# Hybrid decoder step: short TensorE products of the first stage moved apart in a hand-written order table

## The chip, the cores and the metric

The kernel runs on one core of one Trainium2 chip. The metric is device time in microseconds (us), from the first to the last instruction with what lies around them; lower is better. A core has TensorE (matrix products; PE in the rows, its weight loads PEld), VectorE (DVE), ScalarE (ACT), GpSimd (POOL) and SyncE (SP, which here issues transfers). Each engine carries out its own instructions in their order and waits for other engines at semaphores.

## The reference

One layer of a decoder step for a prompt of 2048 tokens and 8 sample tokens, width 1024, cut to what is computed:

```python
xn = _rmsnorm(x, norm1_g)
z = jnp.einsum('btd,de->bte', xn, w_in)
xr, gr, q, k, v = jnp.split(z, IN_SPLITS, axis=-1)
xc, new_conv = _causal_conv(xr, conv_buf, conv_w, conv_b)
hs, h_last = _rglru(xc, h0, gate_a_w, gate_a_b, gate_x_w, gate_x_b, lru_lambda)
rec = hs * jax.nn.gelu(gr)
att = _prompt_attention(q, k, v, attn_sinks)      # window of 128 tokens, softmax with a sink per head
mix = jnp.concatenate([_rmsnorm(rec, rec_norm_g), _rmsnorm(att, attn_norm_g)], axis=-1)
h = x + jnp.einsum('bte,ed->btd', mix, w_out)
hn = _rmsnorm(h, norm2_g)
ff = jax.nn.silu(hn @ w_gate) * (hn @ w_up)
y = _rmsnorm(h + ff @ w_down, final_norm_g)
```

All in float32; the outputs also hold the last keys and values and the last states.

## The kernel before

**Two stages.** The first stage, roughly the first 660 us, does everything up to `mix` and the output projection; the second does the SwiGLU part. Data lies transposed: 128 features on the partitions, tokens along a row. The tokens come in four blocks s = 0 to 3; block 0 has 520 columns (two products of 260), the others 512. Float32 precision comes from splitting both factors into a high and a low part and from three products for each 128 features:

```python
mm(key, out, wh, xh, start=first, stop=False)
mm(key, out, wh, xl, start=False, stop=False)
mm(key, out, wl, xh, start=False, stop=last)
```

**Large products.** `ip{s}_{u}_{i}` is the input projection of block s, column group u; `op{s}_{m}_{i}` the output projection; `o{block}_{kv}_{i}` the attention output. They read 512 columns (260 for s = 0). `g` are the gate products, `s` the attention scores (256 columns).

**Small products.** For each attention block of 128 tokens and each key/value head, `attn_item` makes four scores tiles, the softmax on VectorE and ScalarE (tile `sc`), and then one or two tiles `pt{block}_{kv}_{kb}`, each of **four** 128x128 transposes (helper `tr`, L401) in the one PSUM buffer of `t_tile`. ScalarE casts such a tile (`pth`, L984), VectorE subtracts (`ptl`, L985), and the products `o` read both. So the next `pt` tile can be written only when `ptl` of the one before is done. The other small products are `st_*` (sums for the norms, `rstd_cols`), `bc_*` (their broadcast back, `row_bcast`), `vt` (transposes of V), `dS` (the sample tokens) and `hb`. They share one more PSUM buffer, `m_tile`. Between `st` and `bc` of a norm, VectorE adds a constant (L453) and GpSimd takes a power (L454): the tiles `rccols`, `atcols`. `mix3_0` is the first normed feature group of block 3, written high part first (ScalarE, L868), low part after (VectorE, L869).

**What sets the order.** TensorE's order in the first stage, and a little beyond it, is a table of names, `PE_ORDER`: an entry `key:n` means the next n products of that key. `order_pe` chains them one behind the other, whatever a product waits for, so a product that waits holds all behind it:

```python
for run in PE_ORDER.split():
    key, _, n = run.partition(":")
    for _ in range(int(n or 1)):
        seq.append(todo[key].pop(0))
for a, b in zip(seq, seq[1:]):
    behind(b, a)
```

Entries that begin with `w_` are filler products (`ones` in the rows). The order of the other engines is chosen when the program is built, by a scheduler that simulates all engines with TensorE's order given; seven pairs in `AFTER` are fixed by hand.

Of the kernel before, what the change touches and what calls it, by code (L numbers as in the profile page):

```python
# [120 lines left out]
ip0_2_1:6 s0_1_0:4 s0_1_1:4 ip0_2_1:2 g0_0_0_260 ip0_2_1:13 pt0_0_1:4 ip0_2_1 s1_0_0:4 ip0_2_1:2 ip0_5_0:3 s1_0_1:4
ip0_5_0 g0_0_1_0 ip0_5_0:9 o0_0_0 ip0_5_0:11 ip0_5_1 s1_1_0:4 ip0_5_1:2 pt0_1_1:4 o0_0_0 ip0_5_1:4 g0_0_1_260
ip0_5_1:12 s1_1_1:2 o0_1_0 s1_1_1:2 ip0_5_1:5 ip0_4_0:6 s2_0_0:4 ip0_4_0:3 o0_1_0 ip0_4_0:11 pt1_0_0:4 ip0_4_0:2
s2_0_1:4 ip0_4_0:2 ip0_4_1:24 ip1_8_0:15 ip0_6_0:2 o1_0_0 ip0_6_0:8 pt1_0_1 o1_0_0 pt1_0_1:3 ip0_6_0 ip1_8_0
g0_3_0_0 ip0_6_0:13 ip0_6_1 ip1_8_0:2 ip0_6_1:15 o1_0_1 g0_3_0_260 s2_1_0:4 ip0_6_1 ip1_8_0 ip0_6_1 pt1_1_0
ip0_6_1:5 o1_0_1 s2_1_1:4 pt1_1_0:3 ip0_6_1 ip1_8_0:5 ip1_9_0 g0_3_1_0 ip1_9_0:19 ip0_7_0:9 ip1_9_0:2 pt1_1_1 o1_1_0
pt1_1_1:3 g0_3_1_260 ip1_9_0:2 ip0_7_0:2 o1_1_0 ip0_7_0:13 w_bc_x1_0 bc_x1_0 s3_0_0:3 s3_0_1:4 ip0_7_1 s3_0_0
ip0_7_1 o1_1_1:2 bc_x1_0 w_pt2_0_0:4 ip0_7_1 bc_x1_0 ip0_7_1 bc_x1_0 ip0_7_1:2 pt2_0_0:4 ip0_7_1:18 ip1_10_0:2
o2_0_0:2 pt2_0_1:3 g0_2_0_0 ip1_10_0:12 pt2_0_1 ip1_10_0:10 ip1_11_0:2 o2_0_1 ip1_11_0 s3_1_0:4 pt2_1_0:4 g0_2_0_260
ip1_11_0 s3_1_1:4 ip1_11_0:2 o2_0_1 ip1_11_0:11 g0_2_1_0 pt2_1_1:3 ip1_11_0:7 ip1_4_0:4 o2_1_0 ip1_4_0 pt2_1_1  # L130
ip1_4_0 o2_1_0 g0_2_1_260 ip1_4_0:18 ip1_0_0:2 o2_1_1 ip1_0_0 vt1_0 ip1_0_0:6 dS:2 o2_1_1 pt3_0_0:4 ip1_0_0:5 dS:6
ip1_0_0:6 o3_0_0 ip1_0_0:4 ip1_12_0:2 dS2:2 ip1_12_0:2 pt3_0_1 o3_0_0 ip1_12_0:2 pt3_0_1:3 ip1_12_0:18 ip1_13_0:6
o3_0_1 ip1_13_0:2 o3_0_1 ip1_13_0:3 pt3_1_0:4 ip1_13_0:9 dS3 ip1_13_0 dS3 ip1_13_0:3 ip1_1_0:8 pt3_1_1:2 o3_1_0
pt3_1_1 ip1_1_0:2 pt3_1_1 o3_1_0 dS4:4 s4_0_0 ip1_1_0:2 o3_1_1 s4_0_1:3 s4_0_0:3 s4_0_1 dS4:4 ip1_1_0 o3_1_1
ip1_1_0:11 ip1_5_0:6 dS5:2 s4_1_0:2 s4_1_1:4 ip1_5_0 vt1_1 ip1_5_0:3 s4_1_0:2 ip1_5_0:8 pt4_0_0:2 ip1_5_0 pt4_0_0:2
ip1_5_0:5 ip1_2_0:2 s5_0_0:4 ip1_2_0 s5_0_1:4 ip1_2_0 vt1_2 ip1_2_0:8 o4_0_0 ip1_2_0:6 pt4_0_1 o4_0_0 pt4_0_1:3
ip1_2_0:3 vt1_3 ip1_2_0:3 o4_0_1 s5_1_0:4 s5_1_1:4 o4_0_1 st_rc0 pt4_1_0:4 st_rc0:4 ip1_6_0:15 pt4_1_1:4 bc_rc0_0:3
s6_0_0:4 bc_rc0_0 s6_0_1 ip1_6_0:4 s6_0_1:3 pt5_0_0 bc_rc0_4 pt5_0_0:3 g1_0_0_0 g1_0_1_0 w_st_at0:13 ip1_6_0
st_at0:5 ip1_6_0:4 ip1_3_0:24 ip1_7_0:3 bc_at0_0:4 ip1_7_0:18 bc_at0_4 ip1_7_0:3 op0_0_0:12 op0_0_260:8 g1_1_0_0
op0_0_260:4 op0_1_0:12 op0_0_0 op0_0_260 op0_1_0 op0_0_260:2 op0_0_0:3 op0_1_0:6 op0_0_0:6 op0_1_0:3 op0_0_260:9  # L140
g1_1_1_0 op0_0_0:2 op0_1_0:2 o4_1_0:2 op0_1_260:4 o4_1_1:2 op0_1_260:20 op0_2_0:11 pt5_0_1:4 o5_0_0:2 op0_2_0:13
op0_2_260:13 s6_1_0:3 s6_1_1:4 s6_1_0 op0_2_260:4 o5_0_1 op0_2_260:7 op0_3_0 w_g1_2_0_0:5 g1_2_0_0 pt5_1_0
op0_3_0:12 o5_0_1 op0_3_0:2 pt5_1_0:3 op0_3_0:9 op0_3_260:17 g1_2_1_0 op0_3_260:7 op0_4_0:24 op0_4_260:6 pt5_1_1:4
op0_4_260:2 o5_1_0:2 op0_4_260:16 op0_5_0 o5_1_1 op0_5_0:11 s7_0_0:4 op0_5_0:3 o5_1_1 op0_5_0:4 s7_0_1:4 pt6_0_0:2
op0_5_0:5 op0_5_260:5 pt6_0_0:2 op0_5_260:12 g1_3_0_0 op0_5_260:7 op0_6_0:10 o6_0_0 op0_6_0:3 pt6_0_1 o6_0_0
pt6_0_1:3 op0_6_0:5 g1_3_1_0 op0_6_0:6 op0_6_260:11 s7_1_0 o6_0_1 pt6_1_0:4 s7_1_1:2 op0_6_260 s7_1_1:2 o6_0_1
op0_6_260:2 s7_1_0:3 op0_6_260:10 op0_7_0:24 op0_7_260:3 o6_1_0 bc_x2_0:3 pt6_1_1 o6_1_0 bc_x2_0 op0_7_260 pt6_1_1:3
op0_7_260:11 o6_1_1 op0_7_260:9 ip2_4_0:24 o6_1_1 ip2_0_0:5 pt7_0_0:4 ip2_0_0:10 st_h0:5 ip2_0_0:2 o7_0_0 ip2_0_0:4
o7_0_0 ip2_0_0:3 ip2_5_0:4 pt7_0_1 st_rc1:2 pt7_0_1:3 st_rc1:2 ip2_5_0:9 pt7_1_0:4 ip2_5_0:2 o7_0_1 ip2_5_0:3 o7_0_1
bc_rc1_0:4 ip2_5_0:3 o7_1_0 ip2_5_0:3 pt7_1_1:3 ip2_1_0:2 pt7_1_1 ip2_1_0:8 g2_0_0_0 ip2_1_0:8 o7_1_0 ip2_1_0:4  # L150
o7_1_1 ip2_1_0:2 o7_1_1 g2_0_1_0 ip2_8_0:24 ip2_12_0:18 g2_1_0_0 ip2_12_0:6 ip2_9_0:23 g2_1_1_0 ip2_9_0 ip2_10_0:24
ip2_11_0:18 vt2_0 ip2_11_0:6 ip2_2_0:7 vt2_1 ip2_2_0:17 ip2_13_0:6 vt2_2 ip2_13_0:18 ip2_7_0:7 vt2_3 ip2_7_0:17
ip2_3_0:5 s8_0_0:4 s8_0_1:4 ip2_3_0:2 w_o8_0 ip2_3_0 st_at1:4 ip2_3_0:16 ip2_6_0 s8_1_0:4 s8_1_1 bc_at1_0:4 s8_1_1
pt8_0_0:2 s8_1_1 pt8_0_0 s8_1_1 pt8_0_0 ip2_6_0:7 s9_0_0:4 ip2_6_0:10 g2_2_0_0 ip2_6_0 o8_0_0 s9_0_1:4 ip2_6_0:5
op1_0_0:5 pt8_0_1 op1_0_0:2 o8_0_0 pt8_0_1:3 op1_0_0:4 g2_2_1_0 op1_0_0:13 op1_1_0:3 o8_0_1 op1_1_0:6 s9_1_0:4
op1_1_0:4 s9_1_1:3 op1_1_0 o8_0_1 op1_1_0:5 pt8_1_0:4 s9_1_1 op1_1_0:5 op1_2_0:24 op1_3_0:6 o8_1_0:2 g2_3_0_0
pt8_1_1:4 op1_3_0:18 op1_4_0 g2_3_1_0 op1_4_0:3 o8_1_1 s10_0_0:4 o8_1_1 s10_0_1 pt9_0_0:2 s10_0_1:3 pt9_0_0:2
op1_4_0:20 op1_5_0:3 pt9_0_1:4 op1_5_0 o9_0_0:2 op1_5_0:16 o9_0_1 op1_5_0:4 op1_6_0:2 bc_x3_0:2 s10_1_0 bc_x3_0:2
s10_1_0:3 op1_6_0:2 o9_0_1 op1_6_0 s10_1_1:4 op1_6_0 pt9_1_0:2 op1_6_0:3 pt9_1_0:2 op1_6_0:5 ip3_8_0 op1_6_0 ip3_8_0
op1_6_0 ip3_8_0 op1_6_0 ip3_8_0 op1_6_0 ip3_8_0 op1_6_0 ip3_8_0 op1_6_0 ip3_8_0 op1_6_0 ip3_8_0 op1_6_0 ip3_8_0  # L160
op1_6_0 o9_1_0 op1_6_0 ip3_8_0 pt9_1_1 o9_1_0 ip3_8_0:5 pt9_1_1:3 ip3_8_0:9 op1_7_0 o9_1_1 s11_0_0:3 pt10_0_0:2
op1_7_0:8 s11_0_0 pt10_0_0:2 o9_1_1 s11_0_1 st_rc2:4 s11_0_1 op1_7_0:2 s11_0_1:2 op1_7_0:7 bc_rc2_0:4 op1_7_0:6
ip3_12_0 o10_0_0 ip3_12_0:3 o10_0_0 pt10_0_1:4 ip3_12_0:12 o10_0_1 ip3_12_0:3 s11_1_0:3 ip3_12_0:5 ip3_10_0:8
s11_1_1:4 pt10_1_0 st_h1:4 pt10_1_0:3 s11_1_0 ip3_10_0:4 o10_0_1 ip3_10_0:3 hb_0_0:4 ip3_10_0:6 o10_1_0 ip3_10_0:3
ip3_9_0 pt10_1_1 o10_1_0 pt10_1_1:3 ip3_9_0:8 hb_0_1:4 ip3_9_0:6 o10_1_1 ip3_9_0:9 ip3_11_0:2 o10_1_1 ip3_11_0
# [1564 lines left out]
```

## Time and profile before

| what | value |
|---|---|
| time, median of 3 runs | 2063.03 us (2059.93 to 2065.46) |
| span of the profiled execution | 2054.6 us |
| median of the runs less that span | 8.4 us |
| TensorE, busy share of the span | 98% |
| TensorE, weight loads | 93% |
| VectorE, ScalarE, GpSimd | 71%, 46%, 44% |
| mean granted clock of TensorE | 0.997 |

The profiled execution has no time of its own beside its span, so the 8.4 us are taken as what lies around the span, with a spread of the runs of about 3 us to either side. A busy TensorE is not TensorE at its peak: the ends of its products are modelled, and the starts of the rows are what a distance is read from.

### The profile page before, as it was taken

To read this page: it belongs to the slowest core of one execution; us is meant where nothing else is said; L and a number is where in the kernel's file an instruction comes from. 1 tells how busy PE (TensorE), PEld (TensorE's weight loads), DVE (VectorE), ACT (ScalarE), POOL (GpSimd) and SP (SyncE) were. 2 spreads that over 40 slices of the span, in tenths; PEclk is the share of its full clock that TensorE was granted. 3 is DMA by queue.
4 is the path that set the end of the run, shared out by engine and by line. 5 is a ranking of instruction groups with operands and counts; after the bars stand their busy time and mean duration, and the time that the engine had idled before them with its cause. 6 is when DMAs were issued, how large, how long until landed. Compare 5 with 4: busy or idle time off the path is not lost.

```text
span 2054.6 us, 34857 instructions
## 1 busy us (share of the span) xinstructions
PE 2015.9 (98%) x12319; PEld 1908.1 (93%) x12319; DVE 1459.9 (71%) x2694; ACT 944.6 (46%) x1960; POOL 906.5 (44%) x799
## 2 busy tenths in 40 slices
...
GB/s 329 293 213 143 188 275 159 175 233 210 208 261 280 314 200 223 205 210 207 207 172 210 229 260 258 227 229 221 222 253 265 211 251 189 183 197 196 197 179 96
DMA packets 208991, 450.98 MB, mean 219 GB/s; under 512 B 25232, under 2 KB 82720, under 8 KB 208800
## 3 DMA queue, kind: packets, MB, share of 16 engines
...
## 4 chain that ended last, share of the span: by engine, by line
PE 77%; DVE 9%; DMA 6%; ACT 3%; issue 2%; POOL 1%; SPq 0%; DVEq 0%; ACTq 0%; POOLq 0%
PE ps_u L396 19%; PE ps_g L396 19%; PE pw L396 11%; PE pd L396 10%; PE ip L396 10%; PE op L396 4%; DMA n<-hs 3%; DMA xs<-in_xT 1%; DMA m<-mixed 1%; PE o L396 1%; PE pt L401 1%; DVE sc L974 1%; DVE sc L963 1%; PE s L396 1%; DMA mixed<-n 1%
## 5 line engine op out<-in xcount | busy, mean ns | idle before, releaser
L396 PE MATMUL ps_g<-hn,w_g 128*128 128x342 f32 (+1 forms) x2772 | 489.4, 320 | 4.6 <-DVE c_u L1410 1.8
L396 PE MATMUL ps_u<-hn,w_u 128*128 128x342 f32 (+1 forms) x2772 | 479.9, 319 | 1.9 <-ACT c_u L1436 1.3
L396 PEld LDWEIGHTS ps_g<-hn,w_g 128*128 128x128 f32 x2772 | 445.1, 188 | 6.0 <-DVE c_u L1410 2.3
L396 PEld LDWEIGHTS ps_u<-hn,w_u 128*128 128x128 f32 x2772 | 444.2, 188 | 2.6 <-ACT c_u L1436 1.6
L396 PE MATMUL ip<-xn,w_in 128*128 128x512 f32 (+1 forms) x1680 | 353.4, 358 | 1.9 <-ACT xn L431 1.8
L396 PEld LDWEIGHTS ip<-xn,w_in 128*128 128x128 f32 x1680 | 270.1, 189 | 46.0 <-issue 3.8
L1500 DVE TENSOR_TENSOR y<-y,pw 128x342 f32<-128x342 f32 x504 | 238.7, 504 | 73.0 <-PE pw L396 72.2
L396 PE MATMUL pd<-fh,w_d 128*128 128x344 f32 (+1 forms) x960 | 239.4, 320 | 0.6 <-DVE y L1469 0.6
L396 PE MATMUL op<-mix,w_out 128*128 128x512 f32 (+1 forms) x960 | 203.4, 357 | 0.5 <-DVE rrec L763 0.3
L396 PEld LDWEIGHTS op<-mix,w_out 128*128 128x128 f32 x960 | 155.4, 188 | 29.3 <-issue 5.0
L1469 DVE TENSOR_TENSOR y<-y,pd 128x344 f32<-128x344 f32 (+1 forms) x240 | 117.9, 507 | 75.3 <-PE pd L396 70.7
L396 PEld LDWEIGHTS pd<-fh,w_d 128*128 128x128 f32 x960 | 168.3, 188 | 1.4 <-DVE y L1469 1.1
L396 PE MATMUL pw<-fh,wd 128*128 128x342 f32 x576 | 165.6, 319 | 1.2 <-DVE y L1500 1.2
L396 PE MATMUL pd<-fl,w_d 128*128 128x344 f32 (+1 forms) x480 | 153.4, 320 | 0.0
L1381 DVE TENSOR_TENSOR fl<-c_u,fh 128x342 fp32r<-128x342 f32 (+1 forms) x132 | 107.1, 815 | 48.3 <-ACT fh L1380 47.9
L1225 POOL TENSOR_TENSOR w_u<-ru,w_u 128x512 fp32r<-128x512 f32 x44 | 58.9, 1338 | 181.6 <-ACT w_u L1224 155.0
L1392 POOL TENSOR_TENSOR c_u<-c_u,c_g 128x342 f32<-128x342 f32 (+1 forms) x60 | 60.5, 1008 | 170.7 <-DVE c_u L1410 132.1
L1380 ACT CAST fh<-c_u 128x342 fp32r<-128x342 f32 (+1 forms) x132 | 63.0, 480 | 157.8 <-POOL c_u L1392 61.9
L396 PE MATMUL pw<-t,wd 128*128 128x342 f32 x648 | 126.7, 320 | 2.6 <-DVE t L1381 1.7
L1410 DVE TENSOR_TENSOR c_u<-c_u,ps_u 128x342 f32<-128x342 f32 (+1 forms) x99 | 50.2, 507 | 100.3 <-PE ps_u L396 100.1
L396 PEld LDWEIGHTS pw<-t,wd 128*128 128x128 f32 x648 | 106.0, 188 | 4.4 <-DVE t L1381 2.5
L396 PEld LDWEIGHTS pw<-fh,wd 128*128 128x128 f32 x576 | 105.3, 189 | 1.7 <-DVE y L1500 1.5
...
## 6 DMA issues: line engine op xcount, KB each, us to landing
...
```

Source lines behind the costliest of these rows:

```text
L396: r = nc.tensor.matmul(*args, **kw)
L401: r = nc.tensor.transpose(*args)
L963: seen[f"sm{gb}_{kv}_{g}"] = nc.vector.tensor_tensor_reduce(sc[:, g, :kn], ps[:, gi * 256:gi * 256 + kn], mask[:, k0:k0 + kn], -SCALE, ns[ ...
L974: nc.vector.tensor_scalar(sc[:, g, :kn], sc[:, g, :kn], mx[:, 1, g:g + 1], None, ALU.mult)
L1225: lo_eng.tensor_tensor(w[:, 1, :], src, w[:, 0, :].bitcast(F32), op=ALU.subtract)
L1380: nc.scalar.copy(hi, v)
L1381: nc.vector.tensor_tensor(lo, v, hi.bitcast(F32), ALU.subtract)
L1392: (nc.vector if p == NPAIR - 1 or src is not v else eng(E_MUL[2 * h + n])).tensor_tensor(v, src, g, op=ALU.mult)
L1410: nc.vector.tensor_tensor(o, a, b, op)
L1469: r = nc.vector.tensor_tensor(ys[gi, n, m], ys[gi, n, m], ps, ALU.add)
L1500: nc.vector.tensor_tensor(v, v, ps, ALU.add)
```

## The change

Only the string `PE_ORDER` differs; it grows by 24 lines, so that every later line number is 24 higher in the changed kernel (L396 becomes L420, L401 becomes L425). No instruction is added or removed, and the order of the 3072 large products among themselves stays. Where several small products stood behind one another, the first stays where it is and each of the others goes behind one of the following large (or score or gate) products. Two lines of the table, before and after:

```diff
...
-pt11_0_0:4 ip3_11_0:16 vt3_0 ip3_11_0:5 ip3_13_0:3 pt11_0_1 o11_0_0:2 ip3_13_0 pt11_0_1:3 ip3_13_0:4 vt3_1
...
+ip3_9_0 hb_0_1 ip3_9_0 hb_0_1 ip3_9_0 hb_0_1 ip3_9_0:3 o10_1_1 ip3_9_0:9 ip3_11_0:2 o10_1_1 ip3_11_0 pt11_0_0 ip3_11_0
+pt11_0_0 ip3_11_0 pt11_0_0 ip3_11_0 pt11_0_0 ip3_11_0:13 vt3_0 ip3_11_0:5 ip3_13_0:3 pt11_0_1 o11_0_0:2 ip3_13_0
...
```

Counted from the two tables: 213 small products move later, behind 1 to 8 further large ones (132 transposes of `pt`, 13 `s`, 36 `st`, 15 `bc`, 11 `dS` and 6 `hb`). The places where a small product follows a small one fall from 631 to 454, so 177 are pulled apart. Of the 62 `pt` tiles, 51 have their last transpose later: by one large product in 10, two in 23, three in 11, four in 5, five in 2.

First place, TensorE in block 3 (a name's last number is a buffer number; `ip_11_0` is `ip3_11_0`, `pt_0_0` is `pt11_0_0`), before:

```order
L396 MATMUL o_1_5216<-ptl_1_1_5213,vt_2_4067 128x512
L396 MATMUL ip_11_0_5227<-xn_0_4656,w_in_11_0_5143 128x512
L401 MATMUL pt_0_0_5312<-cs,sc_0_5286 128x128 x4
L396 MATMUL ip_11_0_5227<-xn_1_4661,w_in_11_0_5143 128x512 x3
L396 MATMUL ip_11_0_5227<-xn_2_4666,w_in_11_0_5143 128x512 x3
```

and in the changed kernel:

```order
L420 MATMUL ip_11_0_5227<-xn_0_4656,w_in_11_0_5143 128x512
L425 MATMUL pt_0_0_5312<-cs,sc_0_5286 128x128
L420 MATMUL ip_11_0_5227<-xn_1_4661,w_in_11_0_5143 128x512
L425 MATMUL pt_0_0_5312<-cs,sc_0_5286 128x128
L420 MATMUL ip_11_0_5227<-xn_1_4661,w_in_11_0_5143 128x512
L425 MATMUL pt_0_0_5312<-cs,sc_0_5286 128x128
L420 MATMUL ip_11_0_5227<-xn_1_4661,w_in_11_0_5143 128x512
L425 MATMUL pt_0_0_5312<-cs,sc_0_5286 128x128
L420 MATMUL ip_11_0_5227<-xn_2_4666,w_in_11_0_5143 128x512 x3
```

The run of four transposes has become four single ones; the last of them stands behind three more products of `ip`. This is the commonest form of the change.

Second place, TensorE at the start of the last output projection (full names; `op3_0_0` is the projection of block 3, `st_h2` a norm's sums, `pt15_1_0` a transposed tile of the last attention block), before:

```order
L396 MATMUL op3_2_0_6840<-mix3_0_6289,w_out3_2_0_0_6458 128x512
L396 MATMUL st_h2_6516<-avg_104,hacc2_6025 128x1
L401 MATMUL pt15_1_0_6937<-cs_101,sc15_1_6817 128x128 x4
L396 MATMUL op3_0_0_6468<-mix3_0_6289,w_out3_0_0_0_6406 128x512 x2
L396 MATMUL op3_0_0_6468<-mix3_1_6293,w_out3_0_0_0_6406 128x512 x2
L396 MATMUL st_h2_6516<-avg_104,hacc2_6025 128x1 x3
```

and in the changed kernel:

```order
L420 MATMUL op3_2_0_6840<-mix3_0_6289,w_out3_2_0_0_6458 128x512
L420 MATMUL st_h2_6516<-avg_104,hacc2_6025 128x1
L420 MATMUL op3_0_0_6468<-mix3_0_6289,w_out3_0_0_0_6406 128x512
L425 MATMUL pt15_1_0_6937<-cs_101,sc15_1_6817 128x128
L420 MATMUL op3_0_0_6468<-mix3_0_6289,w_out3_0_0_0_6406 128x512
L425 MATMUL pt15_1_0_6937<-cs_101,sc15_1_6817 128x128
L420 MATMUL op3_0_0_6468<-mix3_1_6293,w_out3_0_0_0_6406 128x512
L425 MATMUL pt15_1_0_6937<-cs_101,sc15_1_6817 128x128
```

The second product of `op3_0_0`, which reads the low part of `mix3_0`, now stands ahead of all four transposes of `pt15_1_0`; before, it stood behind them.

Third place, VectorE near 215 us (`atcols` is the step between the sums and the broadcast of block 0's attention norm, `xc` the convolution, `gt` and `rrec` the gate branch), before:

```order
L842 SCALAR_TENSOR_TENSOR gt_0_2607<-gt_0_2607,rrec 128x512
L453 TENSOR_SCALAR atcols_2792<-st_at_2793 104x5
L786 SCALAR_TENSOR_TENSOR xc_1_2742<-xr_1_2226,vec,xc_1_2742 128x512
L763 TENSOR_TENSOR rrec<-ip_6_0_2859,rb_x_1489 128x512
L786 SCALAR_TENSOR_TENSOR xc_1_2742<-xr_1_2226,vec,xc_1_2742 128x512
L844 SCALAR_TENSOR_TENSOR rrec<-gt_0_2607,rrec 128x512
```

and in the changed kernel:

```order
L866 SCALAR_TENSOR_TENSOR gt_0_2607<-gt_0_2607,rrec 128x512
L810 SCALAR_TENSOR_TENSOR xc_1_2742<-xr_1_2226,vec,xc_1_2742 128x512 x2
L868 SCALAR_TENSOR_TENSOR rrec<-gt_0_2607,rrec 128x512
L787 TENSOR_TENSOR rrec<-ip_6_0_2859,rb_x_1489 128x512
L477 TENSOR_SCALAR atcols_2792<-st_at_2793 104x5
L810 SCALAR_TENSOR_TENSOR xc_1_2742<-xr_1_2226,vec,xc_1_2742 128x512
```

The short step of `atcols` went behind four long ones. Such shifts of single instructions stand all through the first stage on VectorE, ScalarE and GpSimd; the instructions are the same.

## Rows read from the trace of the kernel before

**Rows 1.** The page: the span, and TensorE's busy time.

```profile
span 2054.6 us, 34857 instructions
PE 2015.9 (98%) x12319; PEld 1908.1 (93%) x12319; DVE 1459.9 (71%) x2694; ACT 944.6 (46%) x1960; POOL 906.5 (44%) x799
```

**Rows 2.** Busy time by stretch: each engine's sum over nine stretches, 0 to 700 us.

```profile
sum 700.00, PE 677.70 PEld 575.34 DVE 536.97 ACT 410.68 POOL 198.16; mean PE 75.30 PEld 63.93 DVE 59.66 ACT 45.63 POOL 22.02
```

**Rows 3.** The chain that ended last, from 347 us: start, length, what.

```profile
347.74 10.00 PE ip L396 x43
```

**Rows 4.** Timeline of TensorE, 485 to 492 us: start, length, instruction, count.

```profile
485.45 0.60 PE L401 MATMUL pt<-cs,sc 128*128 128x128 f32 x4
485.81 3.97 PE L396 MATMUL ip<-xn,w_in 128*128 128x512 f32 x16
489.62 0.27 PE L401 MATMUL vt<-cs,vraw 128*128 128x128 f32 x1
489.64 2.11 PE L396 MATMUL ip<-xn,w_in 128*128 128x512 f32 x8
491.59 0.27 PE L401 MATMUL pt<-cs,sc 128*128 128x128 f32 x1
```

**Rows 5.** Timeline of TensorE, 514 to 516 us: single transposes between large products.

```profile
514.63 0.27 PE L401 MATMUL pt<-cs,sc 128*128 128x128 f32 x1
514.66 0.48 PE L396 MATMUL o<-ptl,vt 128*128 128x512 f32 x1
514.98 0.27 PE L401 MATMUL pt<-cs,sc 128*128 128x128 f32 x1
515.32 0.38 PE L401 MATMUL pt<-cs,sc 128*128 128x128 f32 x2
```

**Rows 6.** TensorE's waits to 660 us: for what, us in total, times, longest.

```profile
PE pt L401 <- DVE ptl L985: 3.1, 6, 1.1
PE o L396 <- ACT pth L984: 2.9, 2, 2.1
...
PE o L396 <- DVE ratt L997: 1.2, 2, 0.7
...
PE bc_rc L396 <- POOL rccols L454: 0.7, 1, 0.7
...
PE o L396 <- DVE ptl L985: 0.4, 1, 0.4
```

**Rows 7.** Tile `pth`: what ScalarE idled for ahead of its 62 casts.

```profile
  PE pt L401: 28.8, 21
```

**Rows 8.** Timeline, 425 to 432 us: one `pt` tile and what follows from it.

```profile
425.48 0.38 PE L401 MATMUL pt<-cs,sc 128*128 128x128 f32 x2
...
429.69 0.57 ACT L984 CAST pth<-pt 128x512 fp32r<-128x512 f32 x1
```

**Rows 9.** Timeline, 199 to 202 us: from the sums to the broadcast `bc_rc`.

```profile
199.02 0.15 DVE L453 TENSOR_SCALAR rccols<-st_rc 104x5 f32<-104x5 f32 x1
...
199.25 1.18 POOL L454 TENSOR_TENSOR rccols<-rccols,nhalf 104x5 f32<-104x5 f32 x1 [1.89 <-DVE rccols L453]
...
201.99 0.81 PE L396 MATMUL bc_rc<-cs,rccols 104*128 104x104 f32 x6
```

**Rows 10.** Timeline, 628 to 630 us: transposes of `pt15_1_0`; brackets: idle before, and releaser.

```profile
628.51 0.65 PE L401 MATMUL pt<-cs,sc 128*128 128x128 f32 x4 [0.56 <-DVE ptl L985]
629.10 0.79 PEld L396 LDWEIGHTS op<-mix,w_out 128*128 128x128 f32 x4 [0.18 <-DVE mix L869]
```

**Rows 11.** Timelines, 215 to 224 us: block 0's `atcols` and its broadcast.

```profile
215.77 1.60 POOL L454 TENSOR_TENSOR atcols<-atcols,nhalf 104x5 f32<-104x5 f32 x1 [13.30 <-DVE atcols L453]
...
222.62 1.04 PE L396 MATMUL bc_at<-cs,atcols 104*128 104x104 f32 x8
```

**Rows 12.** By stretch: length, busy us (instructions) of each engine, granted clock, transfers.

```profile
210.00:211.50 1.50, 0.17 (x1) 0.17 (x2) 1.50 (x3) 1.50 (x4) 0.00 (x0) 0.78 0.00 0
211.50:213.00 1.50, 1.50 (x8) 1.50 (x9) 1.50 (x4) 1.50 (x4) 0.00 (x0) 0.50 0.00 0
```

More of the change, by code (lines that the diff above doesn't have):

```diff
@@ L121 @@
[L121 to L165, printed above, removed]
@@ L181 @@
-w_op3_0_0:13 op3_0_0 op3_1_0 o15_0_1 op3_2_0 st_h2 pt15_1_0:4 op3_0_0:4 st_h2:3 op3_0_0 o15_0_1 op3_1_0:3 op3_2_0:3
-op3_0_0:3 op3_1_0:3 op3_2_0:3 op3_0_0:3 pt15_1_1 op3_1_0:3 op3_2_0:3 op3_1_0:2 op3_2_0:2 o15_1_0:2 op3_3_0:3
-pt15_1_1:3 op3_3_0:9 op3_4_0:11 o15_1_1:2 op3_4_0 op3_5_0:12 op3_6_0:12 op3_7_0:12 op3_0_1 op3_1_1 op3_0_1:6
-w_op3_3_1:2 op3_1_1 st_at3 op3_1_1 op3_0_1:3 op3_1_1:3 st_at3:3 op3_0_1:2 op3_1_1:6 op3_3_1:10 bc_at3_0:4 op3_3_1:2
-op3_2_1:12 op3_4_1:12 op3_6_1:12 op3_7_1:12 op3_5_1:12 g0_0_1:12 g0_0_2:12 g0_0_5:12 g0_0_6:12 u0_0_1:12 g0_0_7:12
@@ L186 @@
[L186 to L190 removed]
+ip0_1_0:2 ip0_1_1:2 ip0_12_0:2 ip0_12_1:5 ip0_9_0:5 st_x0 ip0_9_0 st_x0 ip0_9_0 st_x0 ip0_9_0 st_x0 ip0_9_0 st_x0
@@ new lines @@
+ip1_2_0 s5_0_1:4 ip1_2_0 vt1_2 ip1_2_0:8 o4_0_0 ip1_2_0:6 pt4_0_1 o4_0_0 pt4_0_1 ip1_2_0 pt4_0_1 ip1_2_0 pt4_0_1
+ip1_2_0 vt1_3 ip1_2_0:3 o4_0_1 s5_1_0:4 s5_1_1:4 o4_0_1 st_rc0 ip1_6_0 pt4_1_0 ip1_6_0 pt4_1_0 ip1_6_0 pt4_1_0 ip1_6_0
+pt4_1_0 ip1_6_0 st_rc0 ip1_6_0 st_rc0 ip1_6_0 st_rc0 ip1_6_0 st_rc0 ip1_6_0:7 pt4_1_1:4 bc_rc0_0:3 s6_0_0:4 bc_rc0_0
+s6_0_1 ip1_6_0:4 s6_0_1:3 pt5_0_0 bc_rc0_4 pt5_0_0:3 g1_0_0_0 g1_0_1_0 w_st_at0:13 ip1_6_0 st_at0 ip1_6_0 st_at0
+ip1_6_0 st_at0 ip1_6_0 st_at0 ip1_6_0 st_at0 ip1_3_0:24 ip1_7_0:3 bc_at0_0 ip1_7_0 bc_at0_0 ip1_7_0 bc_at0_0 ip1_7_0
```

113 lines of the change are left out of this document (90 added, 23 removed).

## The prediction

> **What bounds the kernel now.** I read the page first, then the busy time by stretch, the chain of waits, the timeline of TensorE in several places, TensorE's list of waits, and last the tiles that the moved products feed. The page puts TensorE at 2015.9 of 2054.6 us busy [rows 1], so the kernel ends when TensorE has worked through its table, and a change counts only by what it does to the distance between the starts of TensorE's products. In the stretch that the table covers, TensorE is marked busy for 677.70 of 700 us [rows 2]: 22.3 us at most are open gaps, and part of those lie at the start and behind the first stage. The chain shows the pace: 43 large products in 10.00 us, 0.2326 us each [rows 3].
>
> **What a small product costs, in a run and alone.** This decides whether pulling them apart pays, and the trace before holds both forms. A run: from the first of four transposes at 485.45 to a single `vt` transpose at 489.62 are 4.17 us, in which 4 small and 16 large products start [rows 4]. The 16 large ones take 16 x 0.2326 = 3.72, which leaves 0.45 for four, 0.112 us each. Alone: from that `vt` at 489.62 to the next transpose at 491.59 are 1.97 us with one small and 8 large products [rows 4]; less 1.86 that leaves 0.11. Alone and in the new pattern, one small behind each large: transposes start at 514.63, 514.98 and 515.32 with one 512-column product between each [rows 5]; two pairs in 0.69 us, less 0.465, leave 0.112 us each. So it is 0.11 us every way.
>
> The rows tempt to another reading. Behind the single transpose at 514.63 the large product is marked as starting only 0.03 us later [rows 5], as if the small one had almost vanished. But the next start is 0.32 us behind that, not 0.23: the large product gives back what the small one seemed to save.
>
> The Trainium skill ("TensorE: Matmul & The Clock Gate", Part 2, step 1, on LDWEIGHTS) says that the next product's weights load while the present one streams. By that rule alone a small product behind a large one would cost only its own columns; with the page's spacing of 56 ns for an isolated 128-column product the 177 places would give 177 x (0.112 - 0.056) = 9.9 us, an estimate from that page. The trace agrees that the small one's own load is hidden, and differs on the sum: its pairs keep 0.112.
>
> **The change part by part.**
>
> *Spacing.* 177 places are pulled apart at a difference of 0.112 - 0.112 = 0. The starts are rounded to 0.01 us, so one pair may be off by 0.005, and the bounds are 177 x 0.005 = 0.9 us to either side. I take 0.
>
> *Results that come later.* 51 of the 62 `pt` tiles have their last transpose later, by 10 x 1 + 23 x 2 + 11 x 3 + 5 x 4 + 2 x 5 = 119 large products, 2.33 on the mean or 0.54 us. What reads the tile starts later by that, if its engine was waiting for it. ScalarE idled until a transpose came ahead of 21 of its 62 casts [rows 7]; ahead of the other 41 it was busy, as at 425 us, where the last transposes start at 425.48 and the cast runs at 429.69 [rows 8]. So about a third of the delays are passed on. They reach TensorE only where it already waits for such a result, or nearly. Five kinds of wait hang on the moved products (`pt` on `ptl`, `o` on `pth`, on `ratt` and on `ptl`, `bc_rc` on `rccols`): 6 + 2 + 2 + 1 + 1 = 12 waits, 8.3 us in all [rows 6]. All twelve lengthened by 0.54, a third of the time: 12 x 21/62 x 0.54 = 2.2 us. The other bound is 0, since products that follow a `pt` run in the table may have moved with it, and TensorE then waits less because it has had the same work to do ahead. I take the middle, **+1.1**.
>
> *The place at 628 us.* TensorE waits 0.56 us for `ptl`, does four transposes, then waits 0.18 for the low part of `mix3_0`, and goes on with `op` from 629.10 [rows 10]. In the changed table the second product of `op3_0_0`, which needs that low part, stands ahead of the transposes. They then begin at about 629.1, not 628.51: four small products that lay in the wait now come behind it, 4 x 0.112 = **+0.5** (bounds 0, if VectorE writes the low part earlier in its new order, and 0.6, the whole of 628.51 to 629.10).
>
> *The sums and broadcasts.* At 199 us the ten sums of `st_rc0` move behind up to eight of the 15 `ip` products that follow them, so that 7 large products and 4 transposes are left ahead of the broadcast `bc_rc`: 7 x 0.2326 + 4 x 0.112 = 2.08 us. VectorE's step starts 0.23 ahead of GpSimd's and that one takes 1.18 [rows 9], 1.41 together; with the start of VectorE some tenths behind the last sum it is 1.6 to 1.8 and fits by about 0.3. I cost it at 0; what hides it is those 2.08 us, and a VectorE that is busy for 0.3 us longer would uncover it, 1 for 1.
>
> *The other engines' order.* Their instructions are the same and only stand elsewhere. The largest shift I found near a norm is the VectorE step of `atcols` behind four instructions. Before, GpSimd's power ends at 215.77 + 1.60 = 217.37 and the broadcast starts at 222.62 [rows 11]: 5.25 us of room, so the four would have to take 1.3 us each to make it late. I cost such shifts at 0 and bound them by the waits that they could remove or double, 8.3 us either way [rows 6].
>
> *The clock.* TensorE fell to the half clock once inside the stage, at 211.5 to 213 us, behind a stretch with 0.17 of 1.5 us of work [rows 12]. Another such gap would cost at most some 1.5 us; I see no place where the change opens one, and take 0.
>
> The sum is 0 + 1.1 + 0.5 = +1.6 us on a span of 2054.6; with the 8.4 us between that span and the median of the runs the time is **2064.6 us**, no change that can be told (0.3%, 6.2 us, is about what a measurement of this kernel can tell from none).
>
> **The rivals.**
>
> *The small products do vanish behind the large ones* (faster). For it: the start of the large product 0.03 us behind the transpose [rows 5]. If each separated product cost that and no more, 177 x (0.112 - 0.03) = 14.5 us would go: 2050.1. Against it: the pairs of the same rows. Chance 0.07.
>
> *The new order of VectorE and ScalarE takes the waits away* (faster). All 8.3 us of those twelve waits gone, with the 0.5 of 628 us: 2054.6 + 0.5 - 8.3 + 8.4 = 2055.2. For it: the scheduler places the instructions anew around transposes that come one at a time. Against it: the same instructions on engines that were late for two thirds of the tiles. It must remove 6.7 us of the 8.3 to count as faster. Chance 0.05.
>
> *The later transposes hold the one `pt` buffer* (slower). Each tile's chain is transposes, cast, subtraction, next tile's transposes, all through one buffer, and `o` behind it. If half of the 51 later tiles pass their 0.54 us on to TensorE, that is 26 x 0.54 = 14.0 us: 2054.6 + 14.0 + 0.5 + 8.4 = 2077.5. For it: TensorE already waits for `ptl` in six places [rows 6], and products that wait hold everything behind them in the table. Against it: the 41 tiles for which ScalarE was busy anyway. It decides from (6.2 - 0.5) / 0.54, so 11 tiles on. Chance 0.27.
>
> **How the numbers follow.** My forecast has 0.61, and the rivals 0.07, 0.05 and 0.27. The range goes from the second rival's 2055 to the third's 2077; it leaves out the first rival and the upper part of the third, together about 0.2, and takes in the bounds of the shifts. The forecast by itself would lie in 2059 to 2069. Faster by over 0.3% are the first two and a little of the forecast, 0.13; slower are the third and a little of the forecast, 0.30; within 0.3% is the rest, 0.57.
>
> **What would show it.** Spacing: in the changed trace, single transposes between large products 0.34 to 0.35 us apart, start to start; 0.26 would mean the first rival. Later results: the five kinds of wait at 8 to 11 us in all; over 14, or ScalarE idling for transposes ahead of far more than 21 casts, means the third; under 2 the second. The place at 628: transposes of `pt15_1_0` first behind a wait for `mix`. The sums: no wait of `bc_rc` much over 0.7. The prediction is wrong if the scheduler's new order makes a long wait where there was none, for a norm's columns or a gate, which no row of before can show.

## The result: slower by 0.38%

| | median | runs | ratio to before, 95% interval |
|---|---|---|---|
| before | 2060.89 us | 6 | |
| changed | 2069.11 us | 6 | 1.0038 [1.0026, 1.005] |

The changed kernel is about 7.8 us slower (0.0038 x 2061). That lies inside the range of 2055 to 2077, but it is not the "no change" that I held likeliest: it is just past the 0.3%, on the slow side, with an interval that begins at 0.26%. The profiled execution of the changed kernel (page: span):

```profile
span 2064.9 us, 34858 instructions
```

The span is 10.3 us longer than in [rows 1]. These spans must be read with care. The runs of the changed kernel have both numbers, and the time is 1.8 us above the span in each (2066.69 for this 2064.9). So the 8.4 us that I put around the span of before were wrong: 2054.6 + 1.8 is 2056.4, a quick execution of a kernel whose runs, in this section and the next, went from 2053 to 2066 us (one more, of 2444.94 us, was in the slow state and is left out). The profiled execution of the changed kernel is the quickest of its six.

**Spacing, as forecast.** TensorE's timeline of the changed kernel, where transposes stand one behind each large product:

```profile
518.13 0.27 PE L425 MATMUL pt<-cs,sc 128*128 128x128 f32 x1
518.16 0.48 PE L420 MATMUL ip<-xn,w_in 128*128 128x512 f32 x1
518.48 0.27 PE L425 MATMUL pt<-cs,sc 128*128 128x128 f32 x1
...
518.82 0.27 PE L425 MATMUL pt<-cs,sc 128*128 128x128 f32 x1
```

The transposes start 0.35 and 0.34 us apart, as in [rows 5]: 0.23 for the large product and 0.11 for the small one.

**The place at 628 us, as forecast.** All engines, changed kernel (what answers to [rows 10]):

```profile
636.52 0.28 PE L420 MATMUL st_h<-avg,hacc 128*128 128x1 f32 x2
638.02 0.50 PE L420 MATMUL op<-mix,w_out 128*128 128x512 f32 x1 [1.22 <-DVE mix L893]
638.36 0.27 PE L425 MATMUL pt<-cs,sc 128*128 128x128 f32 x1
639.74 0.28 PE L420 MATMUL st_h<-avg,hacc 128*128 128x1 f32 x2
```

The transposes now come behind one whole wait of 1.22 us for the low part of `mix3_0`. From one row of `st_h` to the next, 636.52 to 639.74, are 3.22 us with five large products and four transposes between. Before, the rows that answer to them were

```profile
627.68 0.28 PE L396 MATMUL st_h<-avg,hacc 128*128 128x1 f32 x2
...
630.14 0.72 PE L396 MATMUL st_h<-avg,hacc 128*128 128x1 f32 x6
```

630.14 - 627.68 = 2.46 us apart, with four large products and four transposes between. Less 0.23 for the fifth, the place costs 0.53 us, forecast 0.5.

**The sums and the broadcast near 200 us, as forecast** (answers to [rows 9]):

```profile
202.77 1.18 POOL L478 TENSOR_TENSOR rccols<-rccols,nhalf 104x5 f32<-104x5 f32 x1 [3.37 <-DVE rccols L477]
204.48 0.81 PE L420 MATMUL bc_rc<-cs,rccols 104*128 104x104 f32 x6
```

GpSimd's power ends at 203.95 and the broadcast starts at 204.48 without a wait.

**The waits.** TensorE's waits of the changed kernel to 680 us, the largest and those that had been watched (columns as in [rows 6]):

```profile
PE s L420 <- DVE mx L987: 4.1, 5, 3.0
PE o L420 <- ACT pth L1008: 2.8, 3, 1.6
PE o L420 <- DVE ptl L1009: 2.3, 2, 1.5
...
PE pt L425 <- DVE ptl L1009: 1.5, 3, 1.1
```

The five kinds of wait that I had watched did not grow: 2.8 + 2.3 + 1.5 and 1.2 of `bc_rc`, together 7.8 against 8.3 in [rows 6] (`o` on `ratt` is no longer among them). What is new is `s` on `mx`: score products that wait for VectorE's score minima, 4.1 us, of which 2.95 at one place (609.66 us), and a new wait of 1.5 for `ptl` at 542.51.

**The two places.** The chain of waits of the changed kernel from 530 us (start, length, what), its longest pieces:

```profile
529.05 4.13 DMA mixed<-n
533.20 4.37 DMA n<-hs
...
537.67 0.58 DVE n L545
538.24 0.61 DVE gt L866
538.88 0.64 ACT gt L867
...
540.15 0.48 DVE sc L987
...
541.85 0.61 DVE ptl L1009
542.51 0.67 PE o L420
```

and from 590 us:

```profile
596.37 4.95 DMA mixed<-n
601.33 3.22 DMA n<-hs
604.65 0.59 DVE n L545
...
605.78 0.61 DVE q L839
606.41 1.06 ACT q L843
607.50 1.29 DVE ix L846 x2
...
609.66 0.51 PE s L420 x2
```

Both begin at the same pair of transfers: the norm ahead of the second stage stores a tile `mixed`, and only then loads the next tile `n` from `hs`. VectorE, in its order, stands at `n` until the load lands (537.67 and 604.65), and the gate step, the minima and `ptl` stand behind it, with ScalarE's cast behind the gate step. SyncE's own timeline shows what changed in the transfers, at both places alike. Before, both stores of a pair stand ahead of a weight load:

```profile
524.68 1.34 SPq L525 DMA_DIRECT2D mixed<-n  x2
526.12 0.38 SPq L380 DMA_DIRECT2D w_in<-split_w  x1
...
589.59 0.87 SPq L525 DMA_DIRECT2D mixed<-n  x2
590.56 0.40 SPq L380 DMA_DIRECT2D w_out<-split_w  x1
```

and in the changed kernel the second store stands behind it:

```profile
528.16 0.32 SPq L549 DMA_DIRECT2D mixed<-n  x1
528.57 0.38 SPq L404 DMA_DIRECT2D w_in<-split_w  x1
529.05 0.41 SPq L549 DMA_DIRECT2D mixed<-n  x1
...
595.48 0.32 SPq L549 DMA_DIRECT2D mixed<-n  x1
595.85 0.42 SPq L404 DMA_DIRECT2D w_out<-split_w  x1
596.37 0.41 SPq L549 DMA_DIRECT2D mixed<-n  x1
```

The weight loads have 512 KB, the store 172. At the first place the second load of `n` is issued 4.15 us behind the second store (529.05 to 533.20); before it was 1.87 (525.71 to 527.58). The profiles of all kernels here, those of the next section too, agree: 1.9 us in each of the seven with both stores ahead of the weight load, 3.8 to 4.2 in each of the seven with the load between them. At the second place the same stretch is 1.9 to 3.5 us with both stores ahead and 4.0 to 5.0 with the load between (e4, with yet another order there, is left out). SyncE's order never changed alone, so this is seen in the traces and not tested by itself.

At the second place the longer store is only a part of it. In the kernel before, the chain and VectorE's timeline have

```profile
590.14 2.73 DMA mixed<-n
...
592.88 4.74 DMA n<-hs
...
597.71 0.58 DVE n L521
...
599.95 0.47 DVE L963 CUSTOM_DVE_ANT_0 sc<-s,cs,nsk 128x256 f32<-128x256 f32 x1
```

and VectorE's timeline of the changed kernel

```profile
608.71 0.48 DVE L987 CUSTOM_DVE_ANT_0 sc<-s,cs,nsk 128x256 f32<-128x256 f32 x1
```

The store took 4.95 us instead of 2.73, but the load behind it 3.22 instead of 4.74. Taken against the 5.9 us by which this execution is behind at 590 us, `n` is worked on about 1.0 us later than before and the first minimum (608.71) 2.9 later. The other 1.8 us are VectorE's own order: the two `ix`, which wait for ScalarE's `q`, now stand ahead of the four minima, so that these begin 4.06 us behind `n` and not 2.24. At the first place, reckoned in the same way, `n` is worked on 1.6 us later than before and the minima begin 2.5 later; the rest is `rrec`, which waits for ScalarE's gate step and now stands ahead of them.

Behind each wait TensorE's granted clock fell to the half level (by stretch, changed kernel):

```profile
543.00:544.50 1.50, 1.50 (x9) 1.50 (x8) 1.26 (x3) 0.22 (x1) 0.00 (x0) 0.50 0.98 343
544.50:546.00 1.50, 1.50 (x8) 1.32 (x8) 1.36 (x5) 0.99 (x2) 0.00 (x0) 0.50 0.50 202
...
611.00:612.50 1.50, 1.50 (x6) 1.30 (x6) 1.50 (x3) 1.49 (x2) 0.19 (x1) 0.50 0.93 359
612.50:614.00 1.50, 1.50 (x5) 1.11 (x5) 1.50 (x3) 1.50 (x6) 0.19 (x1) 0.50 0.76 295
```

Two stretches of 3 us at half clock. An estimate of what each cost is 1.5 us at most, half of its 3 us, since TensorE is busy all through them; the stretch at 211.5 us of [rows 12] is gone.

**Where the time went.** The start of each product in the table, less its start in the profile of before, shows where an execution falls behind. Medians over the large products within 2 us, in us; the last line is the difference of the spans. The other columns are kernels of the next section.

```
time in   changed  table new,  table old,  before  new order  table new but
before             others old  others new  again   mended     for 4 places
                   (e5)        (e6)        (e9)    (e10)      (e11)
   70       0.0      -0.1        -0.2       -0.1     -0.1       -0.4
  216       1.3       2.3         1.4       -0.8      1.2       -0.9
  300       1.5       2.5         0.8       -1.2      0.6       -1.0
  340       2.1       4.9         1.4       -1.2      1.5       -0.8
  500       1.7       5.6         0.1       -1.4      1.1       -0.8
  530       3.1       5.5         0.7       -1.4      1.1       -0.8
  550       7.5       5.6         4.8       -1.6      1.0       -0.8
  590       5.9       5.4         3.2       -1.6      0.1       -0.4
  612      10.3       5.9         8.5       -2.1      0.5       -0.4
  640       9.4       7.8         6.8       -2.7      3.5       -0.1
  696      10.1       8.6         6.7       -2.7      3.5        0.6
  end      10.3      11.6         7.9        0.8      9.5        3.7
```

The column of the kernel before, profiled again, wanders by up to 2.7 us, so a difference of 1 or 2 us between columns shows little. Up to 500 us the changed kernel is 1.7 us behind, which is within that. It loses 4.4 from 530 to 550 and 4.4 from 590 to 612, the two places; e6 loses 4.1 and 5.3 there.

### The profile page after: what moved, and what is told of

Read it like the earlier page. It is cut to its first block, busy times and chain, and to the rows that moved or that the text cites. A ratio compares the mean times of both kernels' runs of the same rounds, so it can differ in the third digit from the quotient of the medians.

```text
span 2064.9 us, 34858 instructions
## 1 busy us (share of the span) xinstructions
PE 2020.3 (98%) x12319; PEld 1908.2 (92%) x12319; DVE 1455.8 (71%) x2694; ACT 946.2 (46%) x1960; POOL 904.7 (44%) x799
## 4 chain that ended last, share of the span: by engine, by line
PE 79%; DVE 9%; DMA 5%; issue 2%; ACT 2%; POOL 2%; SPq 0%; DVEq 0%; ACTq 0%; POOLq 0%
PE ps_u L420 19%; PE ps_g L420 18%; PE pw L420 10%; PE ip L420 10%; PE pd L420 10%; PE op L420 6%; DMA n<-hs 2%; PE s L420 1%; PE g L420 1%; PE o L420 1%; PE pt L425 1%; DMA mixed<-n 1%; DVE sc L987 1%; DVE hn L602 1%; DMA rd<-in_wdown 1%
## 5 line engine op out<-in xcount | busy, mean ns | idle before, releaser
L420 PE MATMUL ps_g<-hn,w_g 128*128 128x342 f32 (+1 forms) x2772 | 489.5, 320 | 5.0 <-DVE xres L1159 2.1
L420 PE MATMUL ps_u<-hn,w_u 128*128 128x342 f32 (+1 forms) x2772 | 479.8, 319 | 1.2 <-DVE c_g L1434 0.7
L420 PEld LDWEIGHTS ps_g<-hn,w_g 128*128 128x128 f32 x2772 | 445.1, 188 | 6.8 <-DVE c_u L1434 2.4
L420 PEld LDWEIGHTS ps_u<-hn,w_u 128*128 128x128 f32 x2772 | 444.0, 188 | 1.9 <-DVE c_g L1434 1.0
L420 PE MATMUL ip<-xn,w_in 128*128 128x512 f32 (+1 forms) x1680 | 371.1, 364 | 1.9 <-ACT xn L455 1.6
L420 PEld LDWEIGHTS ip<-xn,w_in 128*128 128x128 f32 x1680 | 272.7, 190 | 47.5 <-issue 3.9
L420 PE MATMUL pd<-fh,w_d 128*128 128x344 f32 (+1 forms) x960 | 239.5, 320 | 0.3 <-DVE y L1493 0.2
L420 PE MATMUL op<-mix,w_out 128*128 128x512 f32 (+1 forms) x960 | 210.2, 363 | 1.9 <-DVE mix L893 1.2
L420 PEld LDWEIGHTS op<-mix,w_out 128*128 128x128 f32 x960 | 157.0, 189 | 32.7 <-issue 5.3
L420 PEld LDWEIGHTS pd<-fh,w_d 128*128 128x128 f32 x960 | 168.3, 188 | 1.2 <-DVE y L1493 0.9
L420 PE MATMUL pw<-fh,wd 128*128 128x342 f32 x576 | 165.7, 320 | 1.5 <-DVE y L1524 1.5
L420 PE MATMUL pd<-fl,w_d 128*128 128x344 f32 (+1 forms) x480 | 153.4, 320 | 0.0
L420 PE MATMUL pw<-t,wd 128*128 128x342 f32 x648 | 126.5, 320 | 2.9 <-DVE t L1405 2.3
L420 PEld LDWEIGHTS pw<-t,wd 128*128 128x128 f32 x648 | 106.1, 188 | 4.3 <-DVE t L1405 3.4
L420 PEld LDWEIGHTS pw<-fh,wd 128*128 128x128 f32 x576 | 105.3, 189 | 2.2 <-DVE y L1524 2.1
```

Source lines behind the costliest of these rows:

```text
L420: r = nc.tensor.matmul(*args, **kw)
```

## The experiments

Two theories stood against each other. **Theory O**: the loss comes from the order that the scheduler chose anew for the other engines. **Theory T**: it comes from the table itself, from small products that are separated and later. To part them, an engine's instructions can be chained in any order that was read from a built program:

```diff
+PINNED = {
+    "DVE": """
...
+""",
...
+        def pin_all():
+            by = {i.name: i for i in nc.cur_bb.bb.instructions}
+            for run in PINNED.values():
+                seq = [by[f"I-{n}"] for n in run.split() if f"I-{n}" in by]
+                for a, b in zip(seq, seq[1:]):
+                    tc.add_manual_dep(b, a.name, no_sync, reason="issue order")
...
             order_pe()
-            order_engines()
+            pin_all()
```

The changed kernel's order of VectorE, ScalarE, GpSimd and SyncE differs from that of before in 180 short pieces, in which 2 to 11 instructions are permuted. All ratios below are to the kernel before on the same chip. They are estimated from all runs of both, and are not exactly the quotients of the medians. The median of the kernel before was 2060.41 us beside e1 to e4, 2060.12 beside e5 to e8 and 2058.48 beside e9 to e12; so times of different groups are compared by their ratios.

| kernel | median, us | ratio, 95% interval |
|---|---|---|
| e1 table new, others old, minima free | 2068.48 | 1.0042 [1.0027, 1.0057] |
| e2 table old, others new, minima free | 2066.32 | 1.0029 [1.0018, 1.0039] |
| e3 only `pt` pulled apart | 2067.00 | 1.0036 [1.0023, 1.0049] |
| e4 only the rest pulled apart | 2070.26 | 1.0052 [1.0035, 1.0069] |
| e5 table new, all others old | 2067.22 | 1.0029 [1.0017, 1.004] |
| e6 table old, all others new | 2067.24 | 1.0029 [1.0018, 1.0039] |
| e7 changed, four minima first | 2066.86 | 1.0029 [1.0019, 1.0038] |
| e8 changed, minima and cast first | 2066.70 | 1.0030 [1.0019, 1.0041] |
| e9 before again | 2059.63 | 1.0000 [0.9988, 1.0012] |
| e10 changed, two stretches in old order | 2062.28 | 1.0012 [1.0001, 1.0022] |
| e11 others old, table new but for four places | 2061.61 | 1.0015 [1.0004, 1.0026] |
| e12 table old, two stretches in new order | 2061.74 | 1.0011 [1.0001, 1.0021] |

**e1 and e2: the table and the order apart.** Edit: `pin_all` in the changed kernel with the order of before (e1), and in the kernel before with the order of the changed one (e2).

> TensorE has the changed table; the other four engines are held to the order that they had in the kernel before. Theory O (the loss comes from the order that the scheduler chose anew for VectorE, ScalarE and SyncE): within 0.1% of the kernel before, 2060 to 2064 us. Theory T (the separated and later small products cost it themselves): like the changed kernel, 2068 to 2071 us.

> The reverse: TensorE has the table of before, the other four engines are held to the order that they have in the changed kernel. Theory O: like the changed kernel, 2067 to 2071 us, with TensorE waiting over 3 us for VectorE's score minima near 602 us. Theory T: like the kernel before, 2060 to 2063 us.

Both were slower, by 0.42% and 0.29%. Neither theory alone allows that. In e2 TensorE's wait for the minima was 1.79 us, not over 3. The lists of both lacked the 128 score minima on VectorE, whose place the scheduler still chose; in e1 four of them had come behind the two `ix` near 600 us, as in the changed kernel. So the pair was made again, complete, as e5 and e6.

**e3 and e4: half of the table each.** Edit: in the table of before only `pt` is moved as in the change (e3, 132 products), or only `st`, `bc`, `dS` and `hb` (e4, 68 products); the scheduler is free. The 13 score products that the change moves stay as before in both, though the expectation of e4 names them.

```diff
...
-pt11_0_0:4 ip3_11_0:16 vt3_0 ip3_11_0:5 ip3_13_0:3 pt11_0_1 o11_0_0:2 ip3_13_0 pt11_0_1:3 ip3_13_0:4 vt3_1
+o10_1_1 ip3_9_0:9 ip3_11_0:2 o10_1_1 ip3_11_0 pt11_0_0 ip3_11_0 pt11_0_0 ip3_11_0 pt11_0_0 ip3_11_0 pt11_0_0 ip3_11_0:13
...
```

> Only the pt transposes are pulled apart, the rest of the table is that of before; the other engines' order is chosen anew. Theory T: 132 of 213 moved products, so about 5 of the 8 us, 2066 us. Theory O: nothing proportional; what decides is the order that comes out, anywhere from 2058 to 2070 us.

> The other part alone: st, bc, dS, hb and s products pulled apart, the pt transposes in runs as before. Theory T: about 3 of the 8 us, 2064 us, and with the transposes-only kernel it adds up to the 8 us. Theory O: anywhere from 2058 to 2070 us, and the two need not add up.

Each half costs about as much as the whole, 0.36% and 0.52%, and they do not add up to 0.38%. That speaks against a cost for each moved product, and fits theory O or an order that reacts to any change. The profile of e4, taken of the slowest of its six runs, has a wait that no other profile here has: 5.8 us of `o` for `pth`.

**e5 and e6: the pair, complete.**

> As the first of these kernels, but with all of VectorE held to its order of before; there the 128 score minima (L963 of before) had been left to the scheduler, and near 600 us four of them had come behind the two ix products, as in the changed kernel. Theory O (the other engines' order): 2060 to 2064 us. Theory T (the table itself): 2068 to 2071 us. Theory M (table and order of before fit each other, and either one changed alone breaks the fit): 2066 to 2070 us, without the 3 us wait near 605 us.

> The reverse with all of VectorE held to its order in the changed kernel. Theory O: 2067 to 2071 us. Theory T: 2060 to 2063 us. Theory M: 2066 to 2070 us, with waits of TensorE near 540 and 602 us.

Both are 0.29% slower, and the changed kernel, which has both changes, 0.38% [0.26, 0.50]: less than the 0.58% of the two added up. Of the three theories only M gave these numbers, but what it says of a fit is a reading of them; the two columns above show where each kernel loses. e5 loses 0.1 us from 530 to 550 us and 0.5 from 590 to 612: with the old order the two places are gone. It loses instead in steps of about 1 to 2 us where a moved result is late, above all at 80 to 100, 200, 309 to 323 and 612 to 640 us. TensorE's timeline of e5 at two of them:

```profile
85.48 0.47 PE L749 MATMUL o<-pth,vt 128*128 128x512 f32 x1 [0.97 <-DVE ratt L1357]
...
313.46 0.48 PE L749 MATMUL o<-pth,vt 128*128 128x512 f32 x1 [1.27 <-DVE ratt L1357]
```

The first of these waits stood in the kernel before too (0.74 us, at 84.58) and has grown; at the second TensorE had not waited. What ScalarE idled for ahead of its 62 `pth` casts (columns as in [rows 7]) says the same. In the changed kernel:

```profile
  PE pt L425: 34.9, 24
```

and in e5:

```profile
  PE pt L754: 42.5, 28
```

Before it was 28.8 us at 21 tiles. e6 has the old table and still both places, with waits of 1.31 us for `ptl` and 3.96 for `mx`:

```profile
540.06 0.56 PE L725 MATMUL o<-ptl,vt 128*128 128x512 f32 x1 [1.31 <-DVE ptl L1321]
...
607.88 0.39 PE L725 MATMUL s<-KK,qst 128*128 128x256 f32 x1 [3.96 <-DVE mx L1299]
```

So these two waits are made by the order of the other engines and not by the table.

e1 beside e5 shows one piece of that order by itself. Both have the new table and the old order; only the minima stand elsewhere, near 600 us four of them behind the two `ix` in e1. The transfers of e1 are in the old order, and `n` comes no later than before, against TensorE's own delay there. Still e1 loses 3.5 us from 590 to 612 us by the measure of the columns above, e5 0.5, and e1 has a wait of TensorE for the minima of 2.38 us at 606.74, its longest of that kind (columns as in [rows 6]):

```profile
PE s L744 <- DVE mx L1318: 3.6, 3, 2.4
```

At the second place the minima behind `ix` are thus enough for most of the loss, without a late transfer, as far as one profile of each tells.

**e7 and e8: single swaps.** Edit: all of the changed kernel's order is held, but in one or three pieces.

```diff
 VectorE, 599 us of before (e7, e8)
-ix3_2 ix3_3 sc15_0 sc15_0 sc15_0 sc15_0
+sc15_0 sc15_0 sc15_0 sc15_0 ix3_2 ix3_3
 VectorE, 534 us of before (e8)
-rrec sc13_0 sc13_0 sc13_0 sc13_0 ptl12_0_1
+sc13_0 sc13_0 sc13_0 sc13_0 ptl12_0_1 rrec
 ScalarE, 532 us of before (e8)
-gt3_2 pth12_0_1
+pth12_0_1 gt3_2
```

> The changed kernel with one swap on VectorE, all else held: four score minima of the last attention block ahead of the two ix products again, as before. If the wait of 2.95 us and the half clock behind it come from this swap, about 2 us less than the changed kernel at the end of the stage, 2066 to 2068 us, and no wait of s on mx over 1 us near 605 us. If the waits there come from late loads, 2069 us still.

> The same, and at the other place (535 to 546 us) the cast pth12_0_1 ahead of the gate's second gelu step on ScalarE, and the minima and ptl12_0_1 ahead of rrec on VectorE, as before: three swaps, 14 instructions. Theory O: 4 to 7 us less than the changed kernel, 2062 to 2065 us, and no half clock at 540 to 546 us. Theory T: 2068 to 2070 us.

A gain of 0.08 to 0.09%, less than the intervals can tell. In the trace of e7 the wait of 2.95 us near 605 us has shrunk to 1.05 and the half clock there is gone, but a new wait of 1.76 us (`o` on `ptl`) follows, and 3.0 us are lost from 590 to 612 instead of 4.4. e8 falls behind by 1.7 us near 540 us, where the changed kernel lost 4.4, without a half clock there. But near 605 us its minima still come late, with a wait of TensorE of 2.05 us and a loss of 5.8, because what stands ahead of them is the load of `n` (VectorE's timeline of e8):

```profile
603.18 0.58 DVE L881 SCALAR_TENSOR_TENSOR n<-n,vec,hb 128x344 f32<-128x344 f32 x1 [1.30 <-DMA n<-hs]
```

I had named the instructions that wait behind the transfer, and not the transfer. With e1 this makes two causes at the second place, the minima behind `ix` and the late `n`, and mending the first leaves the second.

**e9: the kernel before again.**

> The kernel before once more, unchanged, for a second profile: whether the span of 2054.6 us was an ordinary execution. Medians of the later runs lie near 2060.5 us, and in runs of other kernels the time is only 1.8 us above the span, so 2054.6 should have been a quick execution, and this span about 2058 us, with the differences at the start of the program or in late loads and not at 540 and 605 us.

The ratio is 1.0000 [0.9988, 1.0012]: the same program beside itself shows no difference, and differences of about 0.1%, as in e10 to e12, are at the edge of what can be told. The span is 2055.4, near that of [rows 1] and not the 2058 that I expected. But the way there differs: 2.7 us ahead at the end of the first stage, and 3.5 us lost again in the second, with the same program. A single profile places a loss well where a wait of microseconds stands in it; a few us of the whole span it does not tell.

**e10: both stretches, with SyncE.** Edit: the changed kernel; in 38 of the 180 pieces (504 to 555 and 587 to 628 us of before, on all four engines) the order of before.

> The changed table; the other engines in the order of the changed kernel, but in two stretches (504 to 555 and 587 to 628 us of before) in that of before. If the loss of the changed kernel is the place near 540 us and the one near 605 us, both of the newly chosen order, about 4 to 6 us less than the changed kernel: 2062 to 2065 us, no wait of o on ptl or of s on mx over 1.5 us there. If late transposes cost the same under any order: 2067 to 2069 us.

The ratio is 1.0012, which on the first batch's 2060.89 us would be 2063.4, inside the first range of the expectation: of the 0.38% are 0.12% left, and the two intervals do not overlap. The waits at both places are gone but for 0.5 us of `s` on `mx` at 601.37; TensorE's row at the first one:

```profile
537.68 0.48 PE L749 MATMUL o<-ptl,vt 128*128 128x512 f32 x1
```

`o` takes `ptl` with no idle time ahead. This profiled execution has a new wait of 2.58 us (`o` on `ratt`, 614.86) and ends 9.5 us behind, but it is the slowest of the kernel's 12 runs, 2065.92 us.

**e11: the table with four places put back.** Edit: e5, and in its table the small products of four stretches stand in runs as before. 144 of the 213 stay moved, and 125 of the 177 places stay pulled apart.

```diff
...
-ip1_2_0 vt1_3 ip1_2_0:3 o4_0_1 s5_1_0:4 s5_1_1:4 o4_0_1 st_rc0 ip1_6_0 pt4_1_0 ip1_6_0 pt4_1_0 ip1_6_0 pt4_1_0 ip1_6_0
-pt4_1_0 ip1_6_0 st_rc0 ip1_6_0 st_rc0 ip1_6_0 st_rc0 ip1_6_0 st_rc0 ip1_6_0:7 pt4_1_1:4 bc_rc0_0:3 s6_0_0:4 bc_rc0_0
+pt4_0_1 ip1_2_0 vt1_3 ip1_2_0:3 o4_0_1 s5_1_0:4 s5_1_1:4 o4_0_1 st_rc0 pt4_1_0:4 st_rc0:4 ip1_6_0:15 pt4_1_1:4
...
```

> All other engines in the order of before; the changed table, but in four stretches (72 to 101, 194 to 206, 304 to 328 and 600 to 641 us of before) the small products stand in runs as before. If the table's own cost is the delay passed on at a few tight places, nearly all of its 6 to 7 us go: 2060 to 2063 us, although most of the products stay pulled apart. If the separation itself costs, most of it stays: 2065 to 2067 us.

It came out between the two: 1.0015, half of e5's 0.29%, though the intervals of the two kernels overlap. In the profile the first stage shows no loss at all against before (-0.1 at 640 us), though against e9 it shows 2.6; the waits at 85 and 313 us are as short as before or gone. So 125 separations and the delays that come with them cost about 3 us (0.8 to 5.4 by the interval). That the four tight places cost as much again is likely and not shown.

**e12: can the gains be had alone?** Edit: the kernel before, with 73 pieces of the new order in 235 to 504 and 555 to 587 us.

> The table of before; the other engines as before, but in two stretches (235 to 504 and 555 to 587 us) in the order of the changed kernel, where the profile of the kernel with the old table and the new order gained time on before (1.1 us near 430, 1.0 and 0.6 us near 565 and 575 us). If these gains hold by themselves: 2 to 3 us less than before, 2057 to 2059 us. If the order of before is worth more as a whole than its parts: 2061 us or more.

No: 1.0011 [1.0001, 1.0021]. Its profile has a wait of 2.7 us of `o` on `ratt`, like that of e10. No kernel of the twelve beats the one before.

## Why the prediction was right or wrong

The number was right to 0.2% and inside the range, but partly by luck. The forecast was a change of +1.6 us and the change measured is +7.8. It stood on the median of three runs, 2063.03; on that of all six, 2060.89, the same sum gives 2062.5, which is 6.6 us below the result and not 4.5. The direction that I held likeliest, no change, was not what came; slower by over 0.3% had 0.30. And by the prediction's own last sign the mechanism was wrong: the new order made long waits where there were none, 2.95 us of `s` on `mx` and 1.52 of `o` on `ptl`, though not for a norm's columns or a gate.

- **Spacing, taken as 0 (bounds 0.9): right.** The pairs stand 0.34 to 0.35 us apart in the changed kernel. The first rival (small products that vanish) is refuted by the same rows. e11 puts what 125 of the 177 separations cost together with their delays at about 3 us.
- **Results that come later, +1.1: mis-sized.** With the other engines held as they were, the table costs 0.29%, about 6 us (e5), for which I had 1.6 with the place at 628 us. At 85 us a wait of my list grew (`o` on `ratt`, 0.74 to 0.97); at 313 us there is one of the same kind, 1.27, where TensorE had not waited, so the twelve waits of before were no bound. In the changed kernel itself little of this is seen (1.7 us by 500 us). That the scheduler built its new order around the later products would explain it; this is argued and not shown. I had treated the two terms as independent.
- **The place at 628 us, +0.5: right**, 0.53 measured.
- **The sums and the broadcast, 0: right**, no wait at 204.48.
- **The other engines' order, "I cost such shifts at 0 and bound them by the waits that they could remove or double": this is the step that failed.** The order by itself costs 0.29% (e6), and putting back two stretches of it takes the changed kernel from 1.0038 to 1.0012 (e10), about 5 us of the 7.8. The bound of 8.3 us held, the 0 did not: I looked for shifts near a norm's columns on VectorE and GpSimd, and not at the four minima that went behind `ix` (e1 beside e5) nor at SyncE's order, where a store and the load behind it moved against weight loads.
- **The clock, 0 (bound 1.5): wrong by two stretches.** At most 1.5 us each at 543 and 611 us, less the one at 211.5 that is gone. Each stands behind a wait, of 1.52 and 2.95 us.
- **The base.** 8.4 us "around the span" are 1.8; the sum is the median of the three runs plus 1.6 all the same, since the span that was too short and the 8.4 that were too many make up that median.
- **The third rival** gave the sign, and e5 shows its mechanism at work; but the changed kernel does not have its mark (the five kinds of wait fell to 7.8 us, and ScalarE idled for transposes ahead of 24 casts, not far more than 21), so its 0.27 was not what came true.

What stays open: the 0.12% of e10 and the 0.15% of e11 above before are not placed, and whether SyncE's order alone, without VectorE's, mends the two places was not tried. At the second one e1 makes it unlikely, since the minima behind `ix` cost 3.5 us there with the old transfers.
